# Differential attention in a hybrid encoder block: two softmax maps joined by one multiply-add, with the first map left undivided

## The chip, the cores and the metric

The kernel runs on one core of one Trainium2 chip. The metric is the device time of one execution in microseconds (us), taken as the median of the runs of one comparison. Profiles show one execution on the same core. Engines are named as in the profile: PE is TensorE (PEld its weight loads), DVE is VectorE, ACT is ScalarE, POOL is GpSimd, SP is the engine that issues the DMAs here.

## What is computed

One encoder block over 1024 tokens and 16 meta tokens, in float32: a norm, projections, two attention branches, gates, an output projection and a SwiGLU feed-forward part. The change touches branch A alone, differential attention with 4 heads:

```python
s1 = einsum('bqhd,bkhd->bhqk', q1, k1) * scale + bias
s2 = einsum('bqhd,bkhd->bhqk', q2, k2) * scale + bias
attn = softmax(s1, axis=-1) - lam * softmax(s2, axis=-1)
y = einsum('bhqk,bkhe->bqhe', attn, v)
# then, over the 128 values of a head
y = y * rsqrt(mean(y * y, axis=-1) + EPS) * subln_g * (1.0 - lambda_init)
```

The bias is minus a slope per head times the distance of the tokens, and `lam` is one number. EPS is 1e-6.

## The kernel before

Every matmul of branch A works on float32 values that are split into a high and a low part, so that three matmuls make one product. Branch A is worked in 32 tiles: 4 heads `h`, and 8 blocks `t` of 128 query rows in each. Below, tile n is n = 8h + t, counted from 0; a row is one query on one SBUF partition, with 1040 keys along it.

For each tile, `scores_a` does the second map first (m = 1), then the first (m = 0). Of each map:

- PE makes the scores in three PSUM banks of 392, 392 and 256 keys (`aps`, L802, two matmuls each).
- DVE reads each bank, adds the distance bias, keeps the running minimum (`amn`) and writes the row to SBUF (`as`, L805; the map 0 rows go to one of two fixed buffers, those of map 1 to a pool of two).
- ACT takes the exponential of the row in place and gives its sum to a column of `adn` (L810).
- DVE takes the reciprocal of that sum (L811).

For m = 1 GpSimd then multiplies the row by the reciprocal and by minus lambda (L813). When both maps are there, DVE does one multiply-add over the row, map 0 times its reciprocal plus the scaled map 1 (L816), and copies the 16 meta columns twice behind the row (L817). In the next tile's time PE transposes the joined row (`apt`, L828, nine transposes in three banks), ACT and DVE split the result (`at`, L831 and L832), and after every second tile PE multiplies by the values (`apy`, L841). After every fourth tile `normed_a` squares the result on ACT, sums the squares on PE (`apst`, L854), divides by 128 and adds EPS on DVE (`af`, L856), takes the power -1/2 on GpSimd (L857), and after three more steps transposes the factors back (`apf`, L862) and applies them (L863).

Between these pieces PE does matmuls of the gates (`pg`, L742), whose weights (`gr` loaded, `gop` split by ACT and GpSimd, L117 and L118) and earlier partial results (`gk`, loaded from `g_d`, added on DVE in L747 and stored again) come by DMA. A buffer of `gk` (three in all) is loaded again only when its last store has been read out.

Order: on PE the order of branch A is written out by hand. Each tile runs a string of 16 slots, `SLOTS = "sgsgsngsgsstntnt"`, where s is a step of the tile's scores, g a quarter of a gate product, n a step of values or norm, t a step of the previous tile's transposes; ten gate quarters stand ahead of each later head (`fill`). DVE, ACT, POOL and SP are ordered by the scheduler of the tile framework, which places them by a simulated timeline; each engine then runs its own list in order. The five score and transpose banks (`SC = 5`) are shared in turn by `aps`, `apt`, `apst` and `apf`, so a late reader on DVE or ACT holds up PE some banks later.

## Time and profile before

| | |
|---|---|
| median of 3 runs | 1446.95 us (1446.73 to 1448.22) |
| the profiled execution | 1446.43 us |
| its span, first to last instruction | 1444.6 us |
| branch A's tiles in it | 326.4 us (first scores) to 598.4 us (last split) |
| PE, DVE, ACT, POOL busy, whole span | 1423.5, 901.6, 679.5, 642.6 us |
| GpSimd scaling (L813) | 32 times, 39.1 us |
| DVE multiply-add (L816) | 32 times, 44.3 us |
| DVE reciprocals (L811) | 64 times, 10.2 us |

How to read it: the span is the core's own; about 1.8 us of an execution's time lie around it. "Idle before" is idle time of the engine just ahead of an instruction, with what ended it. PE's matmuls are pipelined: a row of 0.39 us for 512 columns starts 0.23 us after the one before it at the full clock, so the place in time is read from the starts.

### The profile page before, as it was taken

How to read it: one execution, taken by the hardware profiler on the slowest of the kernel's cores; microseconds unless marked ns; L12 is line 12 of the kernel's file. 1: busy time of each engine (PE TensorE's matmuls, PEld its weight loads, DVE VectorE, ACT ScalarE, POOL GpSimd, SP SyncE). 2: the span in 40 equal slices, each digit the busy share in tenths (PEclk: the TensorE clock that was granted, in tenths of full speed). 3: DMA queues.
4: the chain of work that ended last, by engine and by line, in shares of the span. 5: the costliest groups of instructions: out<-in, count | busy, mean ns of one | idle time of the engine just before them, and what ended most of it. 6: DMA issues, size and time to landing. Idle time of an engine off the chain costs nothing.

```text
span 1444.6 us, 21159 instructions
## 1 busy us (share of the span) xinstructions
PE 1423.5 (99%) x7279; PEld 1221.1 (85%) x7279; DVE 901.6 (62%) x1624; ACT 679.5 (47%) x1290; POOL 642.6 (44%) x605
## 2 busy tenths in 40 slices
PE   8999999999999999999999999999999999999997
PEld 6988989988898989888888878888888888888886
DVE  7478536637697989624614966554555553787567
ACT  6356535545665656545413643333333333444454
POOL 5589227743333333334522665544544552000444
PEclk9999999999999999999999999999999999999999
DMA  8367668995558473586602534333332333964343
GB/s 245 87 211 231 195 160 271 283 289 208 189 168 258 147 226 126 190 255 204 224 32 88 152 103 162 110 102 110 101 103 96 110 102 102 334 205 140 124 130 139
DMA packets 188891, 242.41 MB, mean 168 GB/s; under 512 B 18208, under 2 KB 115936, under 8 KB 188784
## 3 DMA queue, kind: packets, MB, share of 16 engines
q1 hardware_dynamic: 188784, 241.07, 52.5%
q8 instruction: 57, 0.93, 0.3%
q14 instruction: 50, 0.41, 0.1%
HBM read 157.45 MB, written 77.00 MB: 162 GB/s over the span
## 4 chain that ended last, share of the span: by engine, by line
PE 80%; POOL 6%; DVE 5%; issue 4%; DMA 3%; ACT 2%; SPq 0%; POOLq 0%; DVEq 0%; ACTq 0%
PE pg L1299 27%; PE pd L1393 9%; PE pg L742 7%; PE ppa L786 6%; PE po L1076 6%; PE aps L802 3%; PE pp_qb L214 3%; PE apy L841 3%; POOL oa L118 3%; PE pp_ka L214 2%; PE pp_va L214 2%; PE apt L828 2%; PE pp_qa L214 2%; PE bpt L356 1%; PE bpy L362 1%
## 5 line engine op out<-in xcount | busy, mean ns | idle before, releaser
L118 POOL TENSOR_TENSOR wop<-wf,wop 128x512 fp32r<-128x512 f32 x128 | 173.5, 1360 | 164.7 <-ACT wop L117 150.3
L1299 PE MATMUL pg<-t,wop 128*128 128x512 f32 x1056 | 242.6, 389 | 0.0
L1299 PEld LDWEIGHTS pg<-t,wop 128*128 128x128 f32 x1056 | 198.2, 188 | 41.2
L1393 PE MATMUL pd<-ob,oa 128*128 128x512 f32 x924 | 209.9, 389 | 0.4 <-POOL oa L118 0.4
L1393 PEld LDWEIGHTS pd<-ob,oa 128*128 128x128 f32 x924 | 173.3, 188 | 36.8 <-POOL oa L118 0.9
L1299 PE MATMUL pg<-b,wop 128*128 128x512 f32 x792 | 185.6, 392 | 2.3 <-DVE c L1308 2.3
L1299 PEld LDWEIGHTS pg<-b,wop 128*128 128x128 f32 x792 | 149.4, 189 | 34.2 <-issue 2.4
L742 PE MATMUL pg<-hT_hi,gop 128*128 128x512 f32 x384 | 142.9, 397 | 0.0
L118 POOL TENSOR_TENSOR oa<-ra,oa 128x512 fp32r<-128x512 f32 x33 | 44.1, 1337 | 170.0 <-ACT oa L117 168.6
L117 ACT ACTIVATE wop<-wf 128x512 fp32r<-128x512 f32 x128 | 80.2, 631 | 83.3 <-PE pg L1299 47.8
L118 POOL TENSOR_TENSOR gop<-gr,gop 128x512 fp32r<-128x512 f32 x47 | 62.0, 1321 | 105.9 <-ACT gop L117 105.9
L117 ACT ACTIVATE oa<-ra 128x512 fp32r<-128x512 f32 x77 | 48.7, 632 | 106.1 <-PE pd L1393 46.0
L810 ACT ACTIVATE as<-as,amn 128x1040 f32<-128x1040 f32 x64 | 74.5, 1165 | 47.3 <-DVE amn L805 43.2
L1134 DVE TENSOR_TENSOR s<-wf,wf 128x512 f32<-128x512 f32 x22 | 23.7, 1077 | 107.6 <-DMA wf<-in_w_ff_gate_dram 57.4
L802 PE MATMUL aps<-ak,aq 128*128 128x392 f32 (+1 forms) x384 | 90.1, 330 | 0.7 <-DVE amn L805 0.4
L1076 PE MATMUL po<-woh,mT 128*128 128x512 f32 x384 | 88.1, 390 | 0.0
L1076 PEld LDWEIGHTS po<-woh,mT 128*128 128x128 f32 x384 | 71.9, 188 | 14.8
L742 PEld LDWEIGHTS pg<-hT_hi,gop 128*128 128x128 f32 x384 | 72.7, 189 | 11.3 <-DVE gk L747 0.2
L802 PEld LDWEIGHTS aps<-ak,aq 128*128 128x128 f32 x384 | 69.6, 189 | 14.3 <-DVE amn L805 2.0
L343 POOL TENSOR_SCALAR bs<-bs,bdn 128x432 f32<-128x432 f32 (+1 forms) x64 | 41.1, 662 | 87.1 <-DVE bdn L341 74.3
L742 PE MATMUL pg<-hT_lo,gop 128*128 128x512 f32 x192 | 76.1, 396 | 0.0
L813 POOL TENSOR_SCALAR as<-as,adn,neglam 128x1040 f32<-128x1040 f32 x32 | 39.1, 1220 | 63.9 <-DVE adn L811 44.6
(289 smaller groups left out, 3105.9 us busy)
## 6 DMA issues: line engine op xcount, KB each, us to landing
ra<-aop SPq DMA_DIRECT2D x77, 256.0 KB, 2.7
wf<-in_w_ff_gate_dram SPq DMA_DIRECT2D x24, 512.0 KB, 3.8
wf<-in_w_ff_up_dram SPq DMA_DIRECT2D x24, 512.0 KB, 3.9
aop<-as SPq DMA_DIRECT2D x44, 256.0 KB, 2.1
w_c<-in_w_in_dram SPq DMA_DIRECT2D x17, 512.0 KB, 6.1
aop<-c SPq DMA_DIRECT2D x33, 256.0 KB, 2.0
ts_d<-to SPq DMA_DIRECT2D x16, 512.0 KB, 3.4
gw<-in_w_in_dram SPq DMA_DIRECT2D x32, 256.0 KB, 4.2
```

The costliest lines, as they stand in the source:

```text
L117: nc.scalar.activation(hi, src, AF.Copy)
L118: lo_eng.tensor_tensor(lo, src, f32(hi), ALU.subtract)
L214: nc.tensor.matmul(ps[:, :n], a[:, c, :], b[:, c, at:at + n], start=(c == 0 and i == 0), stop=(c == DC - 1 and i == 2))
L343: nc.gpsimd.tensor_scalar(st[:, r, :W], st[:, r, :W], dn[:, r:r + 1], 1.0, ALU.mult, ALU.mult)
L742: nc.tensor.matmul(ps, op[:, a, c], quad(b, *act)[:, c], start=(p in (2, 5, 1) and c == 0 and i == 0), stop=(p in (2, 3, 4) and c == 3 and ...
L786: nc.tensor.matmul(ps, w[:, a, j, :], src(j, b, tk), start=(j == 0 and n == 0), stop=(j == 3 and n == 2))
L802: nc.tensor.matmul(ps[:, :n], qs[m][:, t * P:(t + 1) * P], ks[m][:, vv, k0:k0 + n], start=(vv == 0), stop=(vv == 1))
L810: nc.scalar.activation(s[m][:, 0:L], s[m][:, 0:L], AF.Exp, bias=low, scale=-1.0, accum_out=dn[:, m:m + 1])
L841: nc.tensor.matmul(py[:, cols], v[:kp, a, k, :], at_[:kp, k, b, :], start=(k == 0 and j == 0), stop=(k == 8))
L1076: nc.tensor.matmul(ps, mT[:, c, a, t * P:(t + 1) * P], wos[q, c][:, b], start=(c == 0 and n == 0), stop=(c == DC - 1 and n == 2))
L1299: nc.tensor.matmul(ps, op[:, x, c, :], b[:, y, c, :], start=(p in (1, 2, 5) and c == 0 and n == 0), stop=(p in (4, 2, 3) and c == 3 and n ...
L1393: nc.tensor.matmul(ps[u], oa[:, a, u * P:(u + 1) * P], ob[:, b, :], start=(p in (1, 2, 5) and j == 0 and k == 0), stop=(p in (2, 3, 4) and ...
```

## The change

The first map is no longer divided by its sum. The joined row becomes E0 + E1 * (-lambda * sum0 / sum1), which is the earlier row times sum0 (E0 and E1 are the exponentials of the two maps). The values then come out larger by sum0 in each row, and the norm that follows takes the factor out again, if EPS is multiplied by sum0 squared: sum0 y / sqrt(mean((sum0 y)^2) + EPS sum0^2) = y / sqrt(mean(y^2) + EPS). So the sums of map 0 are kept: four tiles share one small buffer of four columns (`as0` in the constants' pool, three in turn).

```diff
-COMBINE_POOL = (0, 1, 2, 3)
...
+    sums_a = {}
+
     def scores_a(h, t, ld, s):
...
+        if t % 4 == 0:
+            sums_a[h, t // 4] = acon.tile([P, 4], F32, tag="as0", name=f"as0_{nm}", bufs=3)
         dn = small.tile([P, 2], F32, tag="adn", name=f"adn_{nm}")
+        sum_of = (sums_a[h, t // 4][:, t % 4:t % 4 + 1], dn[:, 1:2])
...
-            nc.scalar.activation(s[m][:, 0:L], s[m][:, 0:L], AF.Exp, bias=low, scale=-1.0, accum_out=dn[:, m:m + 1])
-            nc.vector.reciprocal(dn[:, m:m + 1], dn[:, m:m + 1])
+            nc.scalar.activation(s[m][:, 0:L], s[m][:, 0:L], AF.Exp, bias=low, scale=-1.0, accum_out=sum_of[m])
             if m:
-                (nc.gpsimd if t % 4 in COMBINE_POOL else nc.vector).tensor_scalar(
-                    s[1][:, 0:L], s[1][:, 0:L], dn[:, 1:2], neglam, ALU.mult, ALU.mult)
+                nc.vector.reciprocal(dn[:, 1:2], dn[:, 1:2])
+            else:
+                nc.vector.tensor_scalar(dn[:, 0:1], dn[:, 1:2], neglam, sum_of[0], ALU.mult, ALU.mult)
             yield
-        nc.vector.scalar_tensor_tensor(s[0][:, 0:L], s[0][:, 0:L], dn[:, 0:1], s[1][:, 0:L], ALU.mult, ALU.add)
+        nc.vector.scalar_tensor_tensor(s[0][:, 0:L], s[1][:, 0:L], dn[:, 0:1], s[0][:, 0:L], ALU.mult, ALU.add)
...
-        nc.vector.tensor_scalar(f, pst[:, 0:4], 1.0 / P, EPS, ALU.mult, ALU.add)
+        sums = sums_a.pop((h, c))
+        nc.vector.scalar_tensor_tensor(sums, sums, EPS, sums, ALU.mult, ALU.mult)
+        nc.vector.scalar_tensor_tensor(f, pst[:, 0:4], 1.0 / P, sums, ALU.mult, ALU.add)
```

Counted over the kernel: POOL loses its 32 scalings and nothing else (553 listed instructions become 521), DVE has 8 more (1622 become 1630: 32 reciprocals turn into multiplies of the same one-column shape, and 8 squares of the sums come in), ACT and SP have as many as before, and PE's list is the same, instruction for instruction.

The scheduler also places some instructions elsewhere, all of them between the first and the last tile of branch A. Three places matter below. In the lists, `as_..._3180` and `as_..._3181` are the two map 0 rows, `adn` the sums and factors, `aps` score banks, `ISA` DVE's reading of a score bank and of its minimum, `gk_..` gate partials and `pg_..` their banks; line numbers are those of each kernel, and the line of DVE's bank reading is 805 before and 809 now, that of the multiply-add 816 and 820, that of the split of transposes 832 and 836, that of the gates' add 747 and 746.

First place: DVE around the multiply-add of tile 26 (head 3, t = 2), from the first score bank of tile 27 on. Before:

```order
L805 ISA as_3_3_6514,amn_3_6512<-aps_3_1_0_6515,dist,far_a 128x392
L805 ISA amn_3_6512 128x1
L811 RECIPROCAL adn_2_6427<-adn_2_6427 128x1
L805 ISA as_3_3_6514,amn_3_6512<-aps_3_1_392_6522,dist,amn_3_6512 128x392
L805 ISA amn_3_6512 128x1
L816 SCALAR_TENSOR_TENSOR as_0_3180<-as_0_3180,adn_2_6427,as_3_2_6428 128x1040
L832 TENSOR_TENSOR at_0_6234<-apt_1_1_6499,at_0_6234 128x4x128
L747 TENSOR_TENSOR gk_5_6226<-pg_5_6463,gk_5_6226 128x512
L832 TENSOR_TENSOR at_0_6234<-apt_1_2_6506,at_0_6234 16x128
L805 ISA as_3_3_6514,amn_3_6512<-aps_3_1_784_6531,dist_m,amn_3_6512 128x256
```

Now:

```order
L809 ISA as_3_3_6500,amn_3_6498<-aps_3_1_0_6501,dist,far_a 128x392
L809 ISA amn_3_6498 128x1
L836 TENSOR_TENSOR at_0_6221<-apt_1_0_6469,at_0_6221 128x4x128
L809 ISA as_3_3_6500,amn_3_6498<-aps_3_1_392_6508,dist,amn_3_6498 128x392
L809 ISA amn_3_6498 128x1
L818 TENSOR_SCALAR adn_2_6413<-adn_2_6413,neglam,as_3_0_6223 128x1
L746 TENSOR_TENSOR gk_5_6213<-pg_5_6448,gk_5_6213 128x512
L836 TENSOR_TENSOR at_0_6221<-apt_1_1_6485,at_0_6221 128x4x128
L809 ISA as_3_3_6500,amn_3_6498<-aps_3_1_784_6517,dist_m,amn_3_6498 128x256
L809 ISA amn_3_6498 128x1
L836 TENSOR_TENSOR at_0_6221<-apt_1_2_6492,at_0_6221 16x128
L820 SCALAR_TENSOR_TENSOR as_0_3180<-as_3_2_6414,adn_2_6413,as_0_3180 128x1040
```

The multiply-add of tile 26 has moved behind four instructions that it stood ahead of: a gate add, the larger and the smaller of two splits, and the reading of tile 27's third bank.

Which PE instructions these wait for is told by PE's list, the same in both kernels. Here it is from the gate quarter that ends the product `pg_5` on to the transposes of tile 26:

```order
L742 MATMUL pg_5_6463<-hT_hi,gop_5_6223 128x512
L802 MATMUL aps_3_1_784_6531<-ak_1_6166,aq_1_6164 128x256 x2
L742 MATMUL pg_4_6368<-hT_hi,gop_4_6273 128x512
L742 MATMUL pg_4_6368<-hT_lo,gop_4_6273 128x512
L742 MATMUL pg_4_6368<-hT_hi,gop_4_6273 128x512
L802 MATMUL aps_3_0_0_6548<-ak_0_6165,aq_0_6171 128x392 x2
L742 MATMUL pg_4_6368<-hT_hi,gop_4_6273 128x512
L742 MATMUL pg_4_6368<-hT_lo,gop_4_6273 128x512
L742 MATMUL pg_4_6368<-hT_hi,gop_4_6273 128x512
L802 MATMUL aps_3_0_392_6555<-ak_0_6165,aq_0_6171 128x392 x2
L802 MATMUL aps_3_0_784_6559<-ak_0_6165,aq_0_6171 128x256 x2
L828 MATMUL apt_2_0_6565<-ident,as_0_3180 128x128 x4
```

The order of PE has not moved; the last row is the first that needs the multiply-add of tile 26.

Second place: DVE at the first tile of head 2 (tile 16), where two gate adds wait for loads of `gk`. Before:

```order
L747 TENSOR_TENSOR gk_1_5229<-pg_1_5313,gk_1_5229 128x512
L805 ISA as_2_0_5439,amn_0_5437<-aps_0_1_784_5459,dist_m,amn_0_5437 128x256
L805 ISA amn_0_5437 128x1
L805 ISA as_0_3180,amn_0_5437<-aps_0_0_0_5478,dist,far_a 128x392
L805 ISA amn_0_5437 128x1
L811 RECIPROCAL adn_0_5438<-adn_0_5438 128x1
L805 ISA as_0_3180,amn_0_5437<-aps_0_0_392_5487,dist,amn_0_5437 128x392
L805 ISA amn_0_5437 128x1
L805 ISA as_0_3180,amn_0_5437<-aps_0_0_784_5491,dist_m,amn_0_5437 128x256
L805 ISA amn_0_5437 128x1
L747 TENSOR_TENSOR gk_0_5311<-pg_0_5231,gk_0_5311 128x512
```

Now:

```order
L809 ISA as_2_0_5431,amn_0_5428<-aps_0_1_784_5451,dist_m,amn_0_5428 128x256
L809 ISA amn_0_5428 128x1
L746 TENSOR_TENSOR gk_1_5220<-pg_1_5304,gk_1_5220 128x512
L816 RECIPROCAL adn_0_5430<-adn_0_5430 128x1
L809 ISA as_0_3180,amn_0_5428<-aps_0_0_0_5469,dist,far_a 128x392
L809 ISA amn_0_5428 128x1
L809 ISA as_0_3180,amn_0_5428<-aps_0_0_392_5478,dist,amn_0_5428 128x392
L809 ISA amn_0_5428 128x1
L746 TENSOR_TENSOR gk_0_5302<-pg_0_5222,gk_0_5302 128x512
L809 ISA as_0_3180,amn_0_5428<-aps_0_0_784_5482,dist_m,amn_0_5428 128x256
```

The third bank of map 1 is read ahead of the first gate add, but the last bank of map 0 now stands behind the second one.

Third place: SP's DMAs ahead of these two loads. Before:

```order
L751 DMA g_d_75<-gk_0_4938 128x512
L668 DMA aq_0_5378<-qa_d_65 128x1024
L655 DMA ak_0_5372<-ka_d_69 128x1040
L657 DMA ak_0_5372<-ka_d_69 64x1040 x2
L624 DMA gr_3_5531<-in_w_in_dram 128x4x128
L864 DMA ya_d_104<-yg_0_5222 128x512
L636 DMA gk_1_5229<-g_d_77 128x512
L751 DMA g_d_77<-gk_1_5042 128x512
```

Now:

```order
L667 DMA aq_0_5369<-qa_d_65 128x1024
L750 DMA g_d_75<-gk_0_4931 128x512
L654 DMA ak_0_5363<-ka_d_69 128x1040
L656 DMA ak_0_5363<-ka_d_69 64x1040 x2
L623 DMA gr_3_5522<-in_w_in_dram 128x4x128
L870 DMA ya_d_104<-yg_0_5213 128x512
L750 DMA g_d_77<-gk_1_5035 128x512
L635 DMA gk_1_5220<-g_d_77 128x512
```

The store of `gk_0`, whose buffer the load in the last rows takes, goes out behind a load of queries instead of ahead of it, and the load itself goes out behind one more store.

## The prediction

> **What bounds the kernel now.** I read first the page's chain of waits, then the busy time in stretches around the changed tiles, then what PE waits for in branch A, then the changed instructions themselves. The chain is PE's for four fifths, and L813, the scaling, is not among its lines:
>
> ```profile
> PE 80%; POOL 6%; DVE 5%; issue 4%; DMA 3%; ACT 2%; SPq 0%; POOLq 0%; DVEq 0%; ACTq 0%
> PE pg L1299 27%; PE pd L1393 9%; PE pg L742 7%; PE ppa L786 6%; PE po L1076 6%; PE aps L802 3%; PE pp_qb L214 3%; PE apy L841 3%; POOL oa L118 3%; PE pp_ka L214 2%; PE pp_va L214 2%; PE apt L828 2%; PE pp_qa L214 2%; PE bpt L356 1%; PE bpy L362 1%
> ```
>
> In the stretches below (engine busy times, then the granted clock), PE is busy for 243.15 of the 244.95 us that hold nearly all of branch A:
>
> ```profile
> core 0: us, PE busy (x) PEld busy (x) DVE busy (x) ACT busy (x) POOL busy (x), PEclk, DMA share, GB/s
> 336.40:339.60 3.20, 1.26 (x11) 0.97 (x9) 2.98 (x9) 3.06 (x7) 0.45 (x1) 1.00 1.05 404
> 339.64:343.05 3.41, 3.29 (x10) 2.86 (x10) 2.86 (x11) 2.04 (x5) 1.98 (x2) 0.50 1.06 405
> 343.05:588.00 244.95, 243.15 (x1511) 220.60 (x1510) 206.36 (x595) 146.96 (x277) 93.00 (x77) 1.00 0.55 179
> ```
>
> The first two rows are one event: 1.94 us without PE work, and right behind it 3.41 us at half the clock, which lose half of that, 1.7 us. What PE waited for from 324 to 622 us, all of it (total, times, longest):
>
> ```profile
> PE apt L828 <- DVE as L816: 2.6, 2, 1.9
> PE apf L862 <- DVE amn L805: 0.5, 2, 0.3
> PE aps L802 <- DVE amn L805: 0.4, 1, 0.4
> PE apt L828 <- DVE at L832: 0.2, 1, 0.2
> ```
>
> That is 3.7 us, so PE's own order sets the time of this stage, and a change that leaves this order alone can win at most these 3.7 us and the 1.7 of the slow clock, whatever it takes off GpSimd. The rest of the kernel has no changed place on any engine; it can only start earlier or later.
>
> **The change part by part.** The changed instructions (ns: least, median, most), and below them the end of the view of L813, whose list of waiters is empty:
>
> ```profile
> L811 DVE RECIPROCAL adn<-adn x64: 141/160/167, 333.8 to 589.7; 128x1 f32<-128x1 f32 x64
> L813 POOL TENSOR_SCALAR as<-as,adn,neglam x32: 1207/1219/1243, 334.2 to 586.7; 128x1040 f32<-128x1040 f32 x32
> L816 DVE SCALAR_TENSOR_TENSOR as<-as,adn,as x32: 1279/1300/2242, 337.1 to 589.9; 128x1040 f32<-128x1040 f32 x32
> ...
> who waited for it (us, times):
> busy tenths in 40 slices 0000000001111111000000000000000000000000
> ```
>
> *The scaling goes:* 32 x 1.219 = 39 us off POOL. Tile 14 shows why no one waited:
>
> ```profile
> 443.89 1.23 POOL L813 TENSOR_SCALAR as<-as,adn,neglam 128x1040 f32<-128x1040 f32 x1 [1.33 <-DVE adn L811]
> 445.57 0.16 DVE L811 RECIPROCAL adn<-adn 128x1 f32<-128x1 f32 x1
> 445.84 1.30 DVE L816 SCALAR_TENSOR_TENSOR as<-as,adn,as 128x1040 f32<-128x1040 f32 x1
> ```
>
> The scaling ends at 445.12, before even the second reciprocal starts: map 0's exponential comes last. Gain 0. The weight splits on GpSimd, some of which queue behind a scaling, start up to 1.3 us sooner; no gate matmul waits for them in the list above, so 0 again.
>
> *The small instructions:* a one-column multiply by two columns takes the reciprocal's place on the path. The trace has no such row; a reciprocal of the shape takes 0.14 to 0.17 us, so I take no difference, with 0.03 us either way. The same holds for EPS on four columns. The 8 squares of the sums cost DVE at most 8 x 0.17 = 1.3 us; the scheduler puts each behind a multiply-add, and DVE is busy 206 of 245 us, so I take 0; without that cover it is 1.3.
>
> *Tile 0,* whose multiply-add is the longest stall:
>
> ```profile
> 336.85 0.17 DVE L811 RECIPROCAL adn<-adn 128x1 f32<-128x1 f32 x1
> 337.13 1.30 DVE L816 SCALAR_TENSOR_TENSOR as<-as,adn,as 128x1040 f32<-128x1040 f32 x1
> ...
> 338.48 1.20 PE L828 MATMUL apt<-ident,as 128*128 128x128 f32 x9 [1.94 <-DVE as L816]
> ```
>
> DVE's list is the same up to here, and its last input is the one-column instruction. The stall of 1.94 and the half clock stay: 0.
>
> *Tile 26,* where the multiply-add moves behind four instructions (the first place above). DVE and PE before:
>
> ```profile
> 550.25 0.69 DVE L832 TENSOR_TENSOR at<-apt,at 128x512 fp32r<-128x512 f32 x1 [0.32 <-ACT at L831]
> 550.86 0.62 DVE L805 CUSTOM_DVE_ANT_0 as<-aps,dist,far_a 128x392 f32<-128x392 f32 x1
> ...
> 551.40 0.16 DVE L811 RECIPROCAL adn<-adn 128x1 f32<-128x1 f32 x1
> 551.63 0.63 DVE L805 CUSTOM_DVE_ANT_0 as<-aps,dist,amn 128x392 f32<-128x392 f32 x1
> ...
> 552.18 1.29 DVE L816 SCALAR_TENSOR_TENSOR as<-as,adn,as 128x1040 f32<-128x1040 f32 x1
> 553.40 0.68 DVE L832 TENSOR_TENSOR at<-apt,at 128x512 fp32r<-128x512 f32 x1
> 554.00 0.68 DVE L747 TENSOR_TENSOR gk<-pg,gk 128x512 f32<-128x512 f32 x1
> 554.60 0.27 DVE L832 TENSOR_TENSOR at<-apt,at 16x128 fp32r<-16x128 f32 x1
> 554.80 0.47 DVE L805 CUSTOM_DVE_ANT_0 as<-aps,dist_m,amn 128x256 f32<-128x256 f32 x1
> ...
> 549.81 0.60 PE L802 MATMUL aps<-ak,aq 128*128 128x392 f32 x2
> 551.77 0.40 PE L742 MATMUL pg<-hT_hi,gop 128*128 128x512 f32 x1
> 554.92 0.66 PE L828 MATMUL apt<-ident,as 128*128 128x128 f32 x4 [0.19 <-DVE at L832]
> ```
>
> Now the bank reading comes first, once its matmuls are done (549.81 + 0.60 = 550.41): start 550.46. From the starts above, each passes DVE on after 0.54 (a reading of 392), 0.61 (split), 0.55 (reading), 0.23 (one column), 0.60 (gate add; its last matmul ends at 552.17, ahead of it), 0.60 (split), 0.40 (reading of 256) and 0.20 (small split): 3.73 in all, so the multiply-add starts at 554.19 and ends at 555.48 instead of 553.47. The transposes start 0.05 behind it (338.43 to 338.48 in tile 0): 555.53 instead of 554.92. That is a loss of 0.6 us, at a PE idle of about 0.9. It is bounded by 0 (DVE ahead of this sum) and by 1.6 (the first rival). I take 0.6.
>
> *Tile 16,* head 2, where two gate adds wait for their loads (the second and third place):
>
> ```profile
> 463.77 0.69 DVE L747 TENSOR_TENSOR gk<-pg,gk 128x512 f32<-128x512 f32 x1 [2.64 <-DMA gk<-g_d]
> ...
> 467.94 0.69 DVE L747 TENSOR_TENSOR gk<-pg,gk 128x512 f32<-128x512 f32 x1 [0.29 <-DMA gk<-g_d]
> ...
> 467.06 0.62 PE L802 MATMUL aps<-ak,aq 128*128 128x392 f32 x2 [0.44 <-DVE amn L805]
> ...
> 468.21 0.52 PE L802 MATMUL aps<-ak,aq 128*128 128x392 f32 x2
> ```
>
> The first load is now issued behind one store and one more load, but less DVE work waits behind it: PE's 0.44 us may go (gain 0.4). The last bank of map 0 now waits for the second load. If that lands as late as before, its reading starts at about 467.94 + 0.60 = 468.5 and is read out some 0.5 later, and the second pair of matmuls of the next tile, in whose turn that bank comes, starts at 469.05 instead of 468.2: a loss of 0.85, or more if the loads slip. Its issue stands one place earlier, which speaks for less. Between -0.4 and +0.85 I take the middle, +0.2.
>
> *The sum:* 0 + 0 + 0 + 0.6 + 0.2 = +0.8 us on a span of 1444.6, so 1445.4. With the 1.8 us around it (1446.43 - 1444.6) and the 0.5 by which the median of 1446.95 stands above that execution: **1447.7 us**.
>
> *A rule that bears on the 39 us.* Some of DVE's multiply-adds are stretched, beside a GpSimd split that started first (last two rows); in tile 26 (first row) the split came second and was itself the longer one:
>
> ```profile
> 552.97 1.68 POOL L118 TENSOR_TENSOR gop<-gr,gop 128x512 fp32r<-128x512 f32 x1 [0.98 <-ACT gop L117]
> ...
> 560.58 1.29 POOL L118 TENSOR_TENSOR gop<-gr,gop 128x512 fp32r<-128x512 f32 x1 [1.99 <-ACT gop L117]
> 560.72 2.24 DVE L816 SCALAR_TENSOR_TENSOR as<-as,adn,as 128x1040 f32<-128x1040 f32 x1
> ```
>
> The Trainium skill, "SBUF — State Buffer", section "SBUF: two separate sides", says that DVE and GpSimd share one pair of ports as an exclusive lock: whoever starts first holds it for the whole instruction, and a DVE instruction with two SBUF inputs then stands still. These rows agree (2.24 instead of 1.30, done 1.1 us after the split). By that rule the scalings held the lock 39 us, and their removal would free DVE by as much as met it; the trace lets none of it meet a multiply-add, and PE's waits would cap the gain at 3.7 us all the same.
>
> **The rivals.**
>
> *The lock at tile 26, and the clock behind it (slower).* If the split of 552.97 there starts just ahead of the later multiply-add, the multiply-add loses another 0.94 (2.24 - 1.30), PE's idle reaches that of tile 0 (1.94), and the half clock of the second row of the stretches follows: 1.6 + 1.7 = 3.3, so 1450.2 us. It decides from an end of the multiply-add at about 556.4 on. Against it: that split follows its ACT part, which does not move; undisturbed it ends at 552.97 + 1.29 = 554.26, and a multiply-add that is done 1.1 us after it, as in the rows above, is done by 555.4, no later than in my sum. The Trainium skill, "TensorE: Matmul & The Clock Gate", section "Part 1: The HAM clock gate", puts the half clock behind a whole idle window of about 3.4 us that runs freely; here 1.94 us were enough, and the measurement decides.
>
> *The late loads at tile 16 (slower, mostly inside the bound).* If both loads slip by the 1.0 us or so that one more 256 KB store costs, both banks are late: 0.85 + 0.6 for tile 26 + 0.6 more, 1449.0 us.
>
> *The stalls go (faster, inside the bound).* With fewer instructions between scaling and joining, the tiles other than 0 might never be late: 3.7 - 1.94 = 1.8 us gained, 1445.2 us. For it: two of PE's four kinds of wait end with the joined row or the banks around it. Against it: the last input was never the scaling.
>
> *The slow stretch behind tile 0 does not come (faster).* If the multiply is a little shorter than the reciprocal, or the stall falls otherwise, the clock may not drop: 1.7 gained, and with the stalls of the case before 3.5, so 1443.5 us. Against it: nothing ahead of tile 0 has changed.
>
> That the change does not do what it says, so that the time is the same, is no case apart here: the instructions go, and the forecast already says that their going is worth nothing.
>
> **How the numbers follow.** About 0.2%, 2.9 us, is what a measurement of this kernel can tell from no change. Chances: forecast 0.65 (its own range 1446.3 to 1449.0), lock and clock at tile 26 0.12, late loads 0.09, stalls gone 0.09, no slow stretch 0.05. The forecast, the stalls and most of the loads lie within 0.2% of 1446.95: same 0.81. Slower, from 1449.85 on: 0.12 and a quarter of the loads, 0.14. Faster: 0.05. The range that leaves out a tenth on either side takes in the stalls-gone end and the first rival: 1445.0 to 1450.4.
>
> **What would show it.** In the profile after: POOL 39 us less busy, with PE's total waits in this stage still 3 to 5 us; tile 0's stall of 1.9 us and half clock in place; tile 26's transposes about 0.6 us later against the matmuls ahead of them, with an idle row that names the multiply-add; and the scaling's 1.2 us missing nowhere on PE. I am wrong if tile 26 shows no stall, if PE's idle there reaches 1.9 us and a second stretch at half clock follows, if the gate adds of tile 16 hold up PE by more than a microsecond, or if DVE instructions that never met a scaling become shorter.

## The result and the profile after

| | median us | runs | profiled execution us | its span us | POOL busy us | DVE busy us |
|---|---|---|---|---|---|---|
| before | 1448.11 | 14 | 1446.43 | 1444.6 | 642.6 | 901.6 |
| changed | 1451.17 | 14 | 1451.0 | 1449.2 | 602.7 | 904.0 |

The change makes the kernel slower: ratio 1.0023, 95% interval 1.0015 to 1.0031, which is 3.3 us (2.2 to 4.5). A second comparison of the same two kernels, with 12 and 32 runs, gave 1.0020 (1.0009 to 1.0031). 1451.17 lies above the range that was given (1445.0 to 1450.4). Part of that distance is the base: the kernel before had a median of 1446.95 us in the three runs ahead of the prediction and has 1448.11 in these 14, so the same loss on the older base would end at about 1450.2.

The chain of waits after the change is still PE's for four fifths:

```profile
PE 80%; POOL 6%; issue 4%; DVE 4%; DMA 2%; ACT 2%; POOLq 0%; SPq 0%; ACTq 0%; DVEq 0%
```

What PE waited for from 324 to 622 us (total, times, longest), the view that held 3.7 us before:

```profile
PE apt L832 <- DVE as L820: 3.0, 3, 1.6
PE aps L806 <- DVE amn L809: 2.3, 2, 1.9
PE apt L832 <- DVE amn L809: 1.0, 2, 0.6
PE pg L741 <- DVE gk L746: 0.4, 1, 0.4
PE aps L806 <- DMA ak<-ka_d: 0.3, 1, 0.3
```

It now holds 7.0 us. Nearly all of it ends with DVE, although GpSimd lost 39.9 us of work and DVE gained only 2.4. That the 3.3 us more wait equal the loss is chance: these two executions differ by 4.6 us, and in later profiles this view holds 5.6 to 6.2 us for the kernel before (three profiles) and 6.2 to 6.7 for the changed one (three). L820 is the multiply-add, L809 the bank readings, L746 the gate adds. The changed instructions on DVE (ns: least, median, most):

```profile
L816 DVE RECIPROCAL adn<-adn x32: 146/160/166, 334.1 to 591.8; 128x1 f32<-128x1 f32 x32
L818 DVE TENSOR_SCALAR adn<-adn,neglam,as x32: 251/272/277, 337.2 to 595.0; 128x1 f32<-128x1 f32 x32
L820 DVE SCALAR_TENSOR_TENSOR as<-as,adn,as x32: 1278/1298/1840, 337.5 to 595.4; 128x1040 f32<-128x1040 f32 x32
L821 DVE COPY as<-as x32: 148/165/1282, 339.3 to 596.7; 128x32 f32<-128x32 f32 x32
L861 DVE SCALAR_TENSOR_TENSOR as<-as x8: 142/696/1255, 357.8 to 596.6; 128x4 f32<-128x4 f32 x8
```

L861 is the square of the sums: 4 columns, and yet four of the eight took about 1.25 us, nine times the shortest. L818, the one-column product, takes 0.27 us and not the reciprocal's 0.16. L821, the copy of the memory columns, is not part of the change; keep its longest one, 1.28 us, in mind.

The head of head 3 shows what such a square does. Timeline after (start, us, engine and line, idle ahead and what ended it):

```profile
526.19 1.30 DVE L820 SCALAR_TENSOR_TENSOR as<-as,adn,as 128x1040 f32<-128x1040 f32 x1
526.92 1.72 POOL L117 TENSOR_TENSOR gop<-gr,gop 128x512 fp32r<-128x512 f32 x1 [4.55 <-ACT gop L116]
527.41 1.25 DVE L861 SCALAR_TENSOR_TENSOR as<-as 128x4 f32<-128x4 f32 x1
528.59 0.68 DVE L746 TENSOR_TENSOR gk<-pg,gk 128x512 f32<-128x512 f32 x1
...
529.32 0.50 PE L741 MATMUL pg<-hT_hi,gop 128*128 128x512 f32 x1 [0.41 <-DVE gk L746]
```

A GpSimd split (L117) runs from 526.92 to 528.64. The square starts under it and ends 0.02 us behind it. The gate add behind the square is late, and PE waits for that add.

At tile 29 the instruction that stands still is the old copy. Before and after:

```profile
576.64 0.17 DVE L817 COPY as<-as 128x32 f32<-128x32 f32 x1
...
576.76 1.29 POOL L118 TENSOR_TENSOR gop<-gr,gop 128x512 fp32r<-128x512 f32 x1 [3.21 <-ACT gop L117]
```

```profile
580.96 1.29 POOL L117 TENSOR_TENSOR gop<-gr,gop 128x512 fp32r<-128x512 f32 x1 [6.62 <-ACT gop L116]
581.01 1.28 DVE L821 COPY as<-as 128x32 f32<-128x32 f32 x1
...
583.67 0.55 PE L832 MATMUL apt<-ident,as 128*128 128x128 f32 x3 [0.64 <-DVE amn L809]
```

Before, the copy starts 0.12 us ahead of the split and takes 0.17 us. Now it starts 0.05 us behind it and takes 1.28. A shift of 0.17 us between two engines costs 1.1 us of DVE.

Tile 0's stall, and the stretches (busy times of the engines, then the granted clock) that answer to those of before:

```profile
338.84 0.33 PE L832 MATMUL apt<-ident,as 128*128 128x128 f32 x1 [1.60 <-DVE as L820]
```

```profile
340.36:343.77 3.41, 3.41 (x10) 2.92 (x10) 3.26 (x11) 1.68 (x4) 0.35 (x1) 0.50 1.05 394
343.77:592.00 248.23, 242.47 (x1498) 218.70 (x1497) 208.63 (x596) 145.77 (x275) 58.91 (x47) 1.00 0.55 175
```

The half clock is there again. In the long stretch PE is without work for 248.23 - 242.47 = 5.8 us, where it was 1.8 in the first profile of before.

At tile 26 the row that was forecast is there, with the four instructions ahead of the multiply-add:

```profile
557.18 0.48 DVE L809 CUSTOM_DVE_ANT_0 as<-aps,dist_m,amn 128x256 f32<-128x256 f32 x1
557.58 0.27 DVE L836 TENSOR_TENSOR at<-apt,at 16x128 fp32r<-16x128 f32 x1
...
557.79 1.28 DVE L820 SCALAR_TENSOR_TENSOR as<-as,adn,as 128x1040 f32<-128x1040 f32 x1
...
559.12 0.66 PE L832 MATMUL apt<-ident,as 128*128 128x128 f32 x4 [0.71 <-DVE as L820]
```

And at tile 16 both gate adds wait longer for their loads (2.64 and 0.29 us in the first profile of before), and PE waits 1.86 us for the bank behind the second:

```profile
466.00 0.69 DVE L746 TENSOR_TENSOR gk<-pg,gk 128x512 f32<-128x512 f32 x1 [4.05 <-DMA gk<-g_d]
...
470.17 0.69 DVE L746 TENSOR_TENSOR gk<-pg,gk 128x512 f32<-128x512 f32 x1 [2.09 <-DMA gk<-g_d]
```

### The profile page after: what moved, and what is told of

Same layout as the page of the kernel before. It is cut to its first block, busy times and chain, and to the rows that moved or that the text cites. A ratio compares the mean times of both kernels' runs of the same rounds, so it can differ in the third digit from the quotient of the medians.

```text
span 1449.2 us, 21111 instructions
## 1 busy us (share of the span) xinstructions
PE 1424.2 (98%) x7279; PEld 1220.0 (84%) x7279; DVE 904.0 (62%) x1632; ACT 679.7 (47%) x1290; POOL 602.7 (42%) x573
## 4 chain that ended last, share of the span: by engine, by line
PE 80%; POOL 6%; issue 4%; DVE 4%; DMA 2%; ACT 2%; POOLq 0%; SPq 0%; ACTq 0%; DVEq 0%
PE pg L1305 27%; PE pd L1399 9%; PE pg L741 8%; PE ppa L785 6%; PE po L1082 6%; PE aps L806 3%; PE apy L845 3%; PE pp_qb L213 3%; POOL oa L117 3%; PE pp_ka L213 2%; PE pp_va L213 2%; PE apt L832 2%; PE pp_qa L213 2%; PE bpt L355 1%; PE bpy L361 1%
## 5 line engine op out<-in xcount | busy, mean ns | idle before, releaser
L117 POOL TENSOR_TENSOR wop<-wf,wop 128x512 fp32r<-128x512 f32 x128 | 171.6, 1346 | 165.4 <-ACT wop L116 151.6
L117 POOL TENSOR_TENSOR gop<-gr,gop 128x512 fp32r<-128x512 f32 x47 | 64.2, 1367 | 199.9 <-ACT gop L116 191.7
L117 POOL TENSOR_TENSOR oa<-ra,oa 128x512 fp32r<-128x512 f32 x33 | 44.0, 1335 | 170.2 <-ACT oa L116 168.8
L332 DVE CUSTOM_DVE_ANT_0 bs<-bps,tbx,nsink 128x432 f32<-128x432 f32 (+1 forms) x64 | 38.2, 623 | 37.7 <-PE bps L330 28.6
```

What stands on the lines that cost most here:

```text
L117: lo_eng.tensor_tensor(lo, src, f32(hi), ALU.subtract)
```

## The experiments

The theories were: 1, the new order on DVE and SP at tiles 16 and 26; 2, the new arithmetic; 3, the splits on GpSimd, which start at other times without the scalings; then 4, the squares that stand still under a split; and 5, that tile 16 is late by chance.

All kernels issue the same 7,279 matmuls in the same order, so a stretch can be measured from the start of one matmul to the start of a later one. The stretches of the table, each worked out from two start times of one profile: tile 16 (from the 2,622nd matmul, at 445 us before, to the 2,794th), head 3 (2,949th to 3,163rd, 500 to 535 us), tile 26 (3,163rd to 3,319th, to 560), tile 29 (3,430th to 3,566th, 577 to 600), and all from the 2,949th to the 3,566th.

| kernel | ratio to before (95%) | tile 16 | head 3 | tile 26 | tile 29 | 500 to 600 |
|---|---|---|---|---|---|---|
| before, 1st profile | | 29.88 | 35.06 | 24.90 | 23.04 | 100.13 |
| before, 2nd (e9) | 0.9996 (0.9986 to 1.0005) | 30.48 | 35.05 | 24.90 | 23.05 | 100.13 |
| before, 3rd and 4th (e13, e15) | | 30.79, 31.77 | 35.07, 35.05 | 24.89, 24.89 | 23.06, 23.06 | 100.14, 100.13 |
| changed, 1st profile | 1.0023 (1.0015 to 1.0031) | 32.88 | 35.80 | 25.40 | 24.23 | 102.58 |
| changed, 2nd (e10) | 1.0020 (1.0009 to 1.0031) | 32.95 | 35.79 | 25.38 | 24.20 | 102.52 |
| changed, 3rd and 4th (e14, e16) | | 31.31, 30.76 | 35.79, 35.82 | 25.38, 25.38 | 24.21, 24.21 | 102.53, 102.56 |
| e1 one-column product alone | 1.0003 (0.9991 to 1.0015) | 31.33 | 35.07 | 25.36 | 23.05 | 100.60 |
| e2 factor in two small steps | 1.0008 (0.9998 to 1.0018) | 32.81 | 34.92 | 24.84 | 23.04 | 99.94 |
| e3 scaling kept | 1.0020 (1.0009 to 1.0032) | 32.87 | 35.68 | 24.90 | 24.16 | 102.06 |
| e4 no squares | 1.0010 (0.9999 to 1.0021) | 31.29 | 35.12 | 25.38 | 23.03 | 100.68 |
| e5 squares on ScalarE | 1.0010 (1.0000 to 1.0020) | 31.61 | 35.12 | 25.38 | 23.03 | 100.68 |
| e6 as e2, squares on ScalarE | 1.0009 (1.0000 to 1.0017) | 32.06 | 34.92 | 24.82 | 23.05 | 99.94 |
| e8 before without scaling | 1.0002 (0.9994 to 1.0011) | 31.48 | 34.92 | 24.82 | 23.02 | 99.89 |
| e11 as e5, copies on ScalarE | 0.9990 (0.9982 to 0.9999) | 30.92 | 34.92 | 24.82 | 23.03 | 99.92 |
| e12 before, copies on ScalarE | 0.9973 (0.9963 to 0.9984) | 29.81 | 34.87 | 24.77 | 22.82 | 99.58 |
| e18 the same again | 0.9984 (0.9975 to 0.9992) | 31.04 | 34.87 | 24.76 | 22.82 | 99.58 |
| e17 as e11, with e2's factor | 1.0010 (1.0001 to 1.0019) | 30.35 | 34.91 | 24.82 | 23.14 | 100.02 |

Two steady differences lie outside the table. From the 2,450th to the 2,622nd matmul (419 to 445 us before) the four profiles of before take 26.39 to 26.44 us and the four of the changed kernel 25.82 to 25.84, a gain of 0.6 us; e1, e4 and e5, which have its order, take 25.78 to 25.82, and e2, e3, e6 and e8 26.26 to 26.30. PE's wait for `apf` at 419 us (0.27 to 0.29 us in each profile of before) is gone in the changed kernel. And from the start of the last matmul to the end of the span the changed kernel takes 7.7 us in each of its four profiles, every other kernel 7.4 to 7.5; why was not tried.

### One part of the change at a time

The one-column product in the kernel before:

```diff
-            nc.vector.reciprocal(dn[:, m:m + 1], dn[:, m:m + 1])
+            if m:
+                nc.vector.reciprocal(dn[:, m:m + 1], dn[:, m:m + 1])
+            else:
+                nc.vector.tensor_scalar(dn[:, 0:1], dn[:, 1:2], neglam, dn[:, 0:1], ALU.mult, ALU.mult)
```

> The kernel before with one instruction changed: the second reciprocal of each tile becomes the one-column multiply by two columns. Scaling on GpSimd, the join and the constant of the norm stay as before and there are no squares; the factor of the first map is then the product where a quotient belongs. DVE's order of work in branch A is then that of the changed kernel, and SP's order of the gate loads at tile 16 too. Theory 1 (the loss is the rearranged order, set off by this one instruction): 1.5 to 4 us slower than before, with PE's waits behind DVE's bank reading at tile 16 (about 1.9 us) and behind the late multiply-add at tile 26 in place. Theory 2 (the loss is the new arithmetic: squares stretched to as much as 1.25 us): within 0.7 us of before. Theory 3 (the loss comes from GpSimd's splits, which start at other times without the scalings and hold up DVE): within 0.7 us of before.

It multiplies by the first map's sum where the kernel before divides, so its result differs. It brings the new order and with it tile 26's 0.46 us (25.36 against 24.90), but no measurable loss in all: the gain of 0.6 us ahead of tile 16 comes with the same order. The interval ends at 2.2 us, below the 3.3 of the change. Theory 1 alone falls.

The changed kernel with its factor made otherwise:

```diff
                 nc.vector.reciprocal(dn[:, 1:2], dn[:, 1:2])
+                nc.vector.tensor_tensor(dn[:, 1:2], dn[:, 1:2], neglam, ALU.mult)
...
-                nc.vector.tensor_scalar(dn[:, 0:1], dn[:, 1:2], neglam, sum_of[0], ALU.mult, ALU.mult)
+                nc.vector.tensor_tensor(dn[:, 0:1], dn[:, 1:2], sum_of[0], ALU.mult)
```

> The changed kernel, same result, with the factor made in two small steps: the reciprocal's column is multiplied by neglam at once, off the path, and a tensor multiply of two columns stands where the multiply by two columns stood. Scaling stays away and the squares stay. DVE's and SP's order at tiles 16 and 26 is then that of the kernel before; at tiles 21 and 22 the multiply-add moves ahead of three and six instructions. Theory 1: the wait of 1.9 us at tile 16 and the 0.5 at tile 26 go, so 2 to 3.5 us faster than the changed kernel and within 1 us of before. Theory 2: the squares stay, so no more than 0.5 us faster than the changed kernel. Theory 3: the scalings stay away, so the loss of some 3 us stays.

With the old order tile 26's 0.5 us is gone, but so is the loss at head 3 and tile 29, with the squares still there. That is against theory 2 as it stood: squares alone do not cost the time. In this profile one square of eight met a split:

```profile
L862 DVE SCALAR_TENSOR_TENSOR as<-as x8: 139/149/1246, 357.7 to 595.1; 128x4 f32<-128x4 f32 x8
```

The scaling kept, with everything else of the change:

```diff
                 nc.vector.reciprocal(dn[:, 1:2], dn[:, 1:2])
+                nc.gpsimd.tensor_scalar(s[1][:, 0:L], s[1][:, 0:L], dn[:, 1:2], neglam, ALU.mult, ALU.mult)
...
-                nc.vector.tensor_scalar(dn[:, 0:1], dn[:, 1:2], neglam, sum_of[0], ALU.mult, ALU.mult)
+                nc.vector.tensor_copy(dn[:, 0:1], sum_of[0])
```

> The changed kernel with the scaling on GpSimd kept: the second map is scaled as before, the one-column instruction only copies the first map's sum, and join, sums, squares and constant are those of the changed kernel, so the result is the same. All orders on DVE, SP and GpSimd are then those of before, with the squares added. Theory 1: within 0.7 us of before. Theory 2: the squares cost here as they do in the changed kernel, 1.5 to 4 us slower than before. Theory 3: the scalings are back, so within 0.7 us of before.

As slow as the change, in the order of before and with the scalings in place. Theories 1 and 3 both forecast no loss; theory 2's number holds. Head 3 (+0.62 us) and tile 29 (+1.12) are where the loss stands.

The squares taken out:

```diff
-        nc.vector.scalar_tensor_tensor(sums, sums, EPS, sums, ALU.mult, ALU.mult)
-        nc.vector.scalar_tensor_tensor(f, pst[:, 0:4], 1.0 / P, sums, ALU.mult, ALU.add)
+        nc.vector.tensor_scalar(f, pst[:, 0:4], 1.0 / P, EPS, ALU.mult, ALU.add)
```

> The changed kernel without the 8 squares: the norm's constant is EPS alone, so the square of the first map's sum is left out of it. All orders are those of the changed kernel. Theory 1: as slow as the changed kernel within 0.7 us, that is some 3 us slower than before; at most the 0.57 us by which head 3's first gate matmul waited behind a square of 1.25 us comes back. Theory 2: back to before, within 0.7 us. Theory 3: as slow as the changed kernel.

Between the theories: from 500 to 600 us 1.9 us come back (102.58 to 100.68), head 3 and tile 29 are as before, and tile 26's 0.5 us stays. The ratios (1.0023 and 1.0010) differ by as much, but their intervals overlap. The order is nearly that of the changed kernel: without squares on DVE, here and in e5, a reciprocal (499 us) and a split of transposes (574 us) stand sooner in its list than in the changed kernel's.

### The squares elsewhere, and the scaling alone

```diff
-        nc.vector.scalar_tensor_tensor(sums, sums, EPS, sums, ALU.mult, ALU.mult)
+        nc.scalar.activation(sums, sums, AF.Square, scale=EPS ** 0.5)
```

> The changed kernel with one edit: the 8 squares of the sums are taken by ScalarE (a Square with scale the root of EPS, the same result), not by DVE. Orders on DVE, SP and GpSimd stay those of the changed kernel. Theory 4 (the squares cost it, because DVE stands still under a square as long as a GpSimd split beside it runs: four of eight took 1.25 us instead of 0.14): 1.3 to 2.5 us faster than the changed kernel, that is 0.8 to 2 us slower than before, and the waits of PE at the head of head 3 (0.4 us) and at tile 29 (0.6 us) are gone. Theory 1 (the rearranged order at tiles 16 and 26): as slow as the changed kernel within 0.5 us, 3 us slower than before.

Theory 4's numbers, row for row. On ScalarE the square takes 0.21 us every time, and the copy at tile 29 is ahead of the split again:

```profile
L861 ACT ACTIVATE as<-as x8: 196/206/207, 355.6 to 591.7; 128x4 f32<-128x4 f32 x8
```

```profile
577.78 0.17 DVE L821 COPY as<-as 128x32 f32<-128x32 f32 x1
...
578.50 1.30 POOL L117 TENSOR_TENSOR gop<-gr,gop 128x512 fp32r<-128x512 f32 x1 [7.34 <-ACT gop L116]
```

So tile 29's loss belongs to the squares too: it is there with them on DVE (the changed kernel, e3) and gone without (e4, e5). How they make DVE late there shows in e3, where PE, ACT, GpSimd and SP have the lists of before, and DVE has its list of before with the squares added and a one-column copy in place of each tile's second reciprocal. Counted from the 3,319th matmul, DVE and PE of the two kernels run within 0.02 us of each other up to the square behind tile 27's multiply-add, which no split holds. Before, and e3:

```profile
563.84 0.17 DVE L817 COPY as<-as 128x32 f32<-128x32 f32 x1
564.06 0.63 DVE L805 CUSTOM_DVE_ANT_0 as<-aps,dist,amn 128x392 f32<-128x392 f32 x1
```

```profile
567.32 0.15 DVE L862 SCALAR_TENSOR_TENSOR as<-as 128x4 f32<-128x4 f32 x1
...
568.34 0.17 DVE L822 COPY as<-as 128x32 f32<-128x32 f32 x1
568.92 0.63 DVE L809 CUSTOM_DVE_ANT_0 as<-aps,dist,amn 128x392 f32<-128x392 f32 x1 [0.42 <-DVE as L822]
...
581.45 1.27 DVE L822 COPY as<-as 128x32 f32<-128x32 f32 x1
```

Behind the square DVE is 0.08 us late; the bank reading at 568.92 then starts 0.58 us behind the copy instead of 0.22 (why is not shown), and DVE stays 0.4 us late up to tile 29. PE, and with it the split, is only 0.2 us late (17.33 us instead of 17.12 from the 3,319th matmul to the 3,430th). So the copy has lost 0.2 us against the split and starts behind it.

> The changed kernel with both edits that the runs so far speak for: the factor in two small steps, which brings back the order of DVE and SP at tiles 16 and 26, and the squares on ScalarE. Same result. If both parts of the loss are as theories 1 and 4 together have them (0.5 to 1 us of order, 2 us of squares): within 0.7 us of before. If the loss is something else that all undivided joins share (their operands, the place of the sums): 1 to 1.5 us slower than before, like the kernel with the factor in two steps.

1.3 us slower than before, at the edge of what can be told from no change; between 500 and 600 us nothing is lost any more. That is the second case that was expected, a cost that all kernels with the undivided join share: e2, e4, e5 and e6 measured 1.0008 to 1.0010, and e1, e7, e8 and before itself (e9) 0.9996 to 1.0006. None of the first four intervals lies clear of 1.000, and no stretch of the table holds this 1 us; the rival stays open. The extra one-column product was held in seven of its 32 places (0.8 to 1.3 us), as in the kernel with all three edits below.

> The kernel before with 8 squares of four idle columns added on DVE, one ahead of each constant of the norm, whose result nobody reads; nothing else is changed, and the orders stay those of before. Theory 4: 1.3 to 3 us slower than before, with some of the squares at 1.2 us. Theory 1: within 0.7 us of before, since DVE has the time.

This one failed as an experiment. Nothing held the idle squares in place, and they ran at 3.9 to 5.2 us, in the kernel's first microseconds; it counts as one more measurement of before (1.0006, 0.9997 to 1.0014; 100.15 us from 500 to 600).

> The kernel before without its scaling on GpSimd: lambda and the second map's sum are left out, and all else is as before. The order is that of before but for tiles 21 and 22, where the multiply-add moves ahead of three and six instructions. Theory 3 (the splits on GpSimd, set free by the missing scalings, start at other times and hold up DVE): 1.5 to 3.5 us slower than before. Theories 1 and 4: within 0.8 us of before.

This kernel leaves out lambda and the second map's sum. Taking 39 us of GpSimd work away changes nothing that can be measured: the interval ends at 1.6 us, and from 500 to 600 us it is 0.24 us faster than before. Theory 3, which needs 1.5 to 3.5 us, falls.

### The same kernels again, for tile 16

> The kernel before, unchanged, for a second profile and as a measure of the comparison itself. Tile 16's gate loads land late by another amount in every profile so far: seven of the nine other kernels lost 1.4 to 2.3 us there against the first profile of before, whatever their order. Theory 5 (the first profile of before caught tile 16 at its luckiest, and most of the 2.9 us that the changed kernel lost there against it is no effect of the change): the second profile of before loses 1.3 to 2.5 us at tile 16 against the first, and its ratio is 1.000 within 0.001. Theory 1 (tile 16 is late through the rearranged order): it repeats the first within 0.5 us.

> The changed kernel, unchanged, for a second profile. Theories 4 and 5: the fixed part comes back at the same places, 0.5 us at tile 26, 0.5 to 0.7 at the head of head 3 behind a square of 1.25 us, 0.8 to 1.2 at tile 29 behind a copy of 1.28 us; tile 16 loses between 1.3 and 3 us against the first profile of before; the ratio is 1.0015 to 1.003. Theory 1: tile 16 repeats its 3 us within 0.3.

> The kernel before, unchanged, a third profile: what it loses at tile 16 (between 445 and 475 us) and between 500 and 600 us against the first. Theory 5 (tile 16 is late by chance): between 0 and 2.5 us at tile 16; 0.0 within 0.2 us from 500 to 600 us.

> The changed kernel, unchanged, a third profile. Theory 5: between 0.5 and 3 us at tile 16 against the first profile of before. Theory 1 (the order makes tile 16 late): 2.7 to 3.1 us again. Both, through theory 4 and tile 26: 2.4 us within 0.2 from 500 to 600 us.

> The kernel before, unchanged, a fourth profile; as for the third: between 0 and 2.5 us at tile 16, and 0.0 within 0.2 us from 500 to 600 us.

> The changed kernel, unchanged, a fourth profile; as for the third: theory 5 expects between 0.5 and 3 us at tile 16, theory 1 2.7 to 3.1 us; both 2.4 us within 0.2 from 500 to 600 us.

From 500 to 600 us four profiles of before give 100.13 to 100.14 us and four of the changed kernel 102.52 to 102.58: 2.4 us, the same in each. At tile 16 the first profile of before was its fastest of four (29.88 to 31.77), and the changed kernel's four, 30.76 to 32.95, overlap with them. The first two traces differ by 3.0 us there. The second profile of the changed kernel has theory 1's number again (3.07), but 3.4 us at half the clock fall into this stretch (from 467.7 us on, granted clock 0.50), which no other of the eight has there; the third and fourth do not have it (1.43 and 0.88 against the first of before). The means, 30.73 and 31.98, differ by 1.2 us, which four against four with this spread do not settle. (Of the nine other kernels profiled so far six, not seven, lost 1.4 to 2.3 us here; the other three lost 2.9 to 3.0.)

### The copies, and a faster kernel

```diff
-        nc.vector.tensor_copy(s[0][:, L:L + 2 * NM].rearrange("p (a k) -> p a k", a=2),
+        nc.scalar.copy(s[0][:, L:L + 2 * NM].rearrange("p (a k) -> p a k", a=2),
                               s[0][:, S:L].unsqueeze(1).broadcast_to([P, 2, NM]))
```

This line moved in the changed kernel with its squares on ScalarE, and alone in the kernel before:

> The changed kernel with the 8 squares on ScalarE, and the 32 copies of the memory columns (128x32) on ScalarE too, so that of the small instructions of branch A that a GpSimd split can hold up on DVE only the copies' neighbours are left. Same result. In the kernel with the squares alone on ScalarE the copies still stood still for 4.7 us of DVE. If those stalls cost PE what the squares' did: 1 to 2 us faster than that kernel, that is within 0.7 us of before or up to 1 us faster. If DVE has room for them: no change, 1 to 1.5 us slower than before. ScalarE's own queue could cost: up to 1 us slower still.

> The kernel before with only the 32 copies of the memory columns moved from DVE to ScalarE: tells whether a gain in the run above belongs to the copies alone. Same result. If the copies' stalls cost PE: 0.5 to 1.5 us faster than before. If not: within 0.7 us.

> The kernel before with its copies on ScalarE, once more: 2 to 5 us faster than before if the first comparison holds.

With the squares already on ScalarE the move of the copies brings 2.9 us (1.0010 to 0.9990, in two comparisons). Alone it makes the kernel before 3.9 us faster (2.3 to 5.4), and 2.3 (1.2 to 3.6) in the second comparison: 1444.24 and 1444.74 us against 1447.26 and 1447.39. This is the fastest of all the kernels here, and it beats both that were given. How much of this is the copies' stalls is not shown: with the copies gone the scheduler also orders DVE otherwise (in e11 the multiply-add of tile 26 has its old place again, 24.82 against 25.38 us). In e12 and e18 0.55 us of the gain lie from 500 to 600 us and 0.6 from 419 to 445, where the changed kernel's order gains as much. On ScalarE the copy takes 0.2 us and nobody waits for it:

```profile
L817 ACT COPY as<-as x32: 200/218/222, 338.4 to 589.0; 128x32 f32<-128x32 f32 x32
...
who waited for it (us, times):
busy tenths in 40 slices 0000000000000000000000000000000000000000
```

> The changed kernel with all three edits at once: the factor in two small steps (order of before at tiles 16 and 26), the squares on ScalarE and the copies of the memory columns on ScalarE. Same result. If the scaling's absence is worth nothing and the join costs nothing by itself: as fast as the kernel before with its copies on ScalarE, 2 to 4.5 us faster than before. If the extra one-column product on DVE, which took 0.6 to 1.3 us in six or seven of its 32 places, costs PE: 0.5 to 2 us slower than that.

With every cost named so far out of the way, the change is still 3.5 us behind the kernel before with the same copies (medians 1448.21 and 1444.74, one chip). The extra product of two columns, off the path by design, now meets the splits:

```profile
L817 DVE TENSOR_TENSOR adn<-adn,neglam x32: 137/156/1277, 334.2 to 590.0; 128x1 f32<-128x1 f32 x32
...
who waited for it (us, times):
  ACT as L814: 0.5, 2
  PE apt L833: 0.4, 1
```

Seven of the 32 took 0.8 to 1.3 us. They explain 0.4 us of PE directly. Against e12 and e18, 0.44 us lie from 500 to 600 us (100.02 against 99.58) and 0.7 from the 2,794th to the 2,949th matmul (25.37 against 24.67); the rest was not found.

## Why the prediction was wrong

**The scaling, 0:** right. The kernel before without it is within 0.0011 of before.

**The small instructions, "no difference, with 0.03 us either way":** the product by two columns takes 0.11 us more than the reciprocal (0.272 against 0.160), outside what was allowed. Alone it cost nothing that can be measured.

**The 8 squares, "at most 8 x 0.17 = 1.3 us of DVE", of which 0 on the path:** this is the step that failed, in its size and in its cover. They took 8 x 0.697 = 5.6 us of DVE (8 x 0.17 is 1.4), and PE lost 1.9 us to them: 0.7 at head 3, behind a square that a split held, and 1.2 at tile 29, where a copy that the squares had made late was held. The nearest row for a short instruction between SBUF operands was not the reciprocal. It stood in the profile of before, at the code line below the multiply-add:

```profile
L817 DVE COPY as<-as x32: 150/165/1106, 339.0 to 591.4; 128x32 f32<-128x32 f32 x32
```

A most that is seven times the median says that something outside the instruction sets its length. The prediction had the rule at hand (the Trainium skill, "SBUF — State Buffer", section "SBUF: two separate sides": DVE with two SBUF inputs, or in a two-port mode, and GpSimd take the shared ports in turn, for a whole instruction). It applied it to the multiply-adds, which cost 1.3 us anyhow, and not to an instruction of 0.15 us, where it multiplies the price by nine. The cover failed as well: "DVE is busy 206 of 245 us" is a mean, and just behind the multiply-add at the head of head 3 there was no slack of 1.1 us.

**Tile 0, stall and half clock stay:** the stall stayed (1.94 us before, 1.60 now; 1.18 to 1.94 and 1.60 to 1.99 in four profiles each), and the slow stretch came in this profile. That it had to come was not right: see the last section.

**Tile 26, +0.6 us:** right; 0.48 us (25.38 against 24.90), with the row that was named. PE's idle time there was put at about 0.9 us; the rows give 0.19 + 0.6 = 0.8, and it measured 0.71.

**Tile 16, +0.2 us between -0.4 and +0.85:** the middle was too low if the two traces are taken at their word (3.0 us), and the bound with it. But this stretch varies by 1.9 us between profiles of one kernel, so a bound from a single trace could not be had; 1.2 us is the difference of the means.

**The sum:** steady from profile to profile are +0.5 (tile 26), +1.9 (squares), -0.6 (419 to 445 us) and +0.3 (behind the last matmul), together 2.1 us, against a measured 3.3 (2.2 to 4.5) and 2.9 (1.3 to 4.5). The -0.6 belongs to a moved place that the prediction did not look at. A difference of 1.2 us at tile 16 would close the sum, but it is not settled; the rest can also lie ahead of branch A, where profiles of one kernel differ by as much. It stays open. The forecast's own range, 1446.3 to 1449.0, is not what its bounds give: with 0 to 1.6 for tile 26 and -0.4 to +0.85 for tile 16 it would be 1446.5 to 1449.4.

**The rivals:** "the lock at tile 26" had the mechanism and looked for it at the wrong instruction: the multiply-add there took 1.28 us. "The late loads" are part of what tile 16 shows. Of the stalls that might go, the one behind `apf` went, which is part of the 0.6 us; the one of 0.7 us at tile 30 stayed.

**What was to show it:** PE's waits of 3 to 5 us are 7.0, but the kernel before has up to 6.2 in other profiles, so this sign could not tell; POOL is 39.9 us less busy, as said; the scaling's 1.2 us is missing nowhere on PE. "DVE instructions that never met a scaling become shorter" was listed as a sign of error, and it came: the 32 multiply-adds took 44.3 us before and 42.0 in the changed kernel, their most fell from 2.24 to 1.84. It is the new order, not the missing scalings, that sets them beside fewer splits: with the scalings and the new order (e1) they took 42.2 us, with the old order and no scalings (e8) 44.2.

## What to carry to other kernels

Before a short DVE instruction between SBUF operands is added to a stage in which GpSimd works, look at the most, not the median, of the short ones that are there; price it at the length of a GpSimd instruction for each time that they can meet, or give it to ScalarE. An instruction that is not held itself can still make a later one start behind such a GpSimd instruction, as at tile 29 in e3. Work taken off an engine that nobody waits for buys nothing, and the instructions that replace it can land on one that is waited for. Where a stretch is bound by how fast loads come, look at several executions before a difference between two traces is explained.

## What the runs showed that was not expected

Which short DVE instructions a GpSimd split holds up: squares of 4 columns (two SBUF inputs, up to 1.26 us), products of two single columns (1.28) and copies of 32 columns (one input, 1.28) were held. Of 64 reciprocals of one column before, 19 began while a GpSimd instruction ran (nine of them under a split) and none took more than 0.17 us; products by two columns (e1: eight, at most 0.27) and one-column copies (e3: nine, at most 0.15) were not held either; the constant of the norm, whose input comes from PSUM, began under a split four times of eight in the changed kernel and took 0.16. In all profiles here together 144 of the squares, of the products of two single columns and of the 32-column copies took over 0.4 us: each began while a GpSimd split ran and ended 0.01 to 0.04 us behind it. None that began outside a split took over 0.19. The Trainium skill's rule cited above agrees with the squares, the products, the reciprocals and the constant; for the copy, with one input, it needs the two-port mode, which by the same section a float32 copy from SBUF to SBUF brings about; no run here shows the mode itself.

The same stall does not always bring the slow clock. In the third profile of before PE waits 1.94 us at tile 0, as in the first. The matmul there, and the stretch behind it, with the granted clock in the third column from the right:

```profile
338.72 0.33 PE L828 MATMUL apt<-ident,as 128*128 128x128 f32 x1 [1.94 <-DVE as L816]
```

```profile
338.70:342.10 3.40, 3.26 (x19) 2.81 (x20) 3.25 (x11) 3.07 (x7) 2.46 (x2) 1.00 1.05 405
```

The clock stays at 1.00. A stretch of 3.4 us at half clock can also come elsewhere: between 834 and 844 us two of the four profiles of each kernel have one, and the part from the 3,566th matmul to the last takes 837.0 to 837.3 us with it and 835.9 to 836.1 without, so executions of one kernel differ by 1.1 us there. In the clock records of the traces the times between two changes are whole multiples of 3.413 us (334.51 is 98 of them, 491.52 is 144). Behind tile 0, of four profiles of before one has the half clock. Of four of the changed kernel three have it, after stalls of 1.60, 1.97 and 1.99 us, and one has not, after 1.80; what decides was not tried. The Trainium skill, "TensorE: Matmul & The Clock Gate", section "Part 1: The HAM clock gate", has windows that run freely, so that a stall is counted by where it falls in them; these rows fit that, though not its whole idle window of 3.4 us.
